# Weight sums of a seven-product matmul moved to the stages before it, and its first row tiles prepared inside the last block of the product before

## The chip, the cores and the metric

The kernel runs on one core of a Trainium2 chip. The metric is the device time of one execution in microseconds (us); three timed executions of the kernel before stand below, and beside them one execution with a profile. The engines are TensorE (PE, with its weight loads PEld), VectorE (DVE), ScalarE (ACT), GpSimd (POOL) and the queue of SyncE (SP). DMAs are issued by SP, POOL and ACT.

## The reference

One layer of a hybrid decoder, for 1024 prompt positions and 8 samples of one position (1032 tokens), all in fp32:

```python
    z = x @ w_in + b_in                      # 1024 -> 3584
    y_a = s5_mixer(u_a, ...)                 # scan, GELU, GLU
    y_b = u_b * spatial_mix(layer_norm(v_b), sgu_w, sgu_b)
    merged = (jax.nn.sigmoid(gate_a) * (y_a @ w_branch_a)
              + jax.nn.sigmoid(gate_b) * (y_b @ w_branch_b))
    mix = merged @ w_out + b_out
    x1 = layer_norm(DN_ALPHA * x + mix, ln1_g, ln1_b)
    ff = jnp.square(jax.nn.relu(x1 @ w_up + b_up)) @ w_down + b_down
    ple = jax.nn.sigmoid(x1 @ w_ple_gate + b_ple_gate) * (p @ w_ple)
    x2 = layer_norm(DN_ALPHA * x1 + ff + ple, ln2_g, ln2_b)
```

`w_up` is 1024 x 4096 and `w_down` 4096 x 1024; the change lies around these two products.

## The kernel before

**Layout and precision.** Features lie on the 128 partitions, tokens along the free axis: a tile is 128 x 1032, a half of it 516, a quarter 258. Every fp32 operand is split into a high part (a copy that rounds, mostly on ACT) and a low part (a subtraction on DVE), and a product is three matmuls: high by high, high by low, low by high. Weights come through the pool `raw` (loaded by SP), are split into the pool `hl` of four buffers, and the splits run three weight tiles ahead of PE.

**Stages.** In order: `w_in` (to about 380 us, with the scan beside it), `glu` (four tiles, to 410.6), `pab` (the two branch products, eight times a product `psB` and a product `psA` of 36 matmuls each, to about 505), `out` (twice eight), `pg` and `ple`, then from 715.1 the first feed-forward product ("up"), from 1069.6 the second ("down"), and a normalisation that ends at 1422. In `pab` the sum of a tile m is `sb = psB * sb; sa = psA * sa; sa = sa + sb` on DVE, then a split; the two PSUM buffers alternate, so the `psA` of the next tile needs this tile's `sa = psA * sa` done.

**The two feed-forward products** use a scheme of seven products in the place of eight block products (P1 to P7). Up runs 16 blocks `up_pair(p)`. A block is seven products of 24 matmuls (168 in all) into three PSUM regions; its four weight tiles (t = 0 to 3) are `w_up` pieces and sums of pieces, made on DVE by `up_prep`. Some products add into a region that holds an earlier one: P6, P7 and P4 go onto P1, so P4 may start only when DVE has read the result of P7 (`hB[:, 1]`, line 1314). Each block's result h goes, as seven operands, into DRAM tiles `hd` through POOL's queue.

**Down** runs seven products of four units `dn_unit(pi, mp)` of 96 matmuls. Its row operands (`hop`, 23 buffers) are loaded from `hd` into `hraw` (four buffers) by SP, and split. Its weights are pieces of `w_down` and the sums S1 to S4 of such pieces, which `dn_sums` forms: eight steps of four loads of 512 KB (SP), four DVE operations of 128x1024 and four stores of 512 KB to DRAM (POOL). One step of the generator is taken at each product of up (`next(dsums, None)`). The residual `acc`, parked in DRAM (`accd`), is loaded again by SP before down starts, and the result of P1 is added to it in P1.

**What sets the order.** Each engine and each DMA queue does its instructions in the order of the program that the tile framework's scheduler wrote; a tile whose buffer is taken again waits for the last reader, a DMA included.

Of the kernel before, what the change touches and what calls it, by code (L numbers as in the profile page):

```python
# [10 lines left out]
F32 = mybir.dt.float32  # L11
# [46 lines left out]
def hybrid_step_kernel(ctx: ExitStack, tc: tile.TileContext, i, o):  # L58
# [7 lines left out]
    rawp = ctx.enter_context(tc.tile_pool(name="raw", bufs=4))  # L66
# [843 lines left out]

    yhl += [(unit(f"A{8 + 2 * m}", F32R, name=f"yh{m + 2}"), unit(f"A{9 + 2 * m}", F32R, name=f"yl{m + 2}"))
# [5 lines left out]
    for m in range(4):  # L917
# [9 lines left out]
        split(yb[m][0], yb[m][1], ubt[m])  # L927

# [15 lines left out]
    for m in range(8):  # L944
# [11 lines left out]
        mg.append((a, b))  # L956

# [125 lines left out]
    lnx = bpool.tile([128, 1024], F32, tag="dsz", name="lnx")  # L1083
# [30 lines left out]
    for j, (p_, m) in enumerate(passes):  # L1114
# [83 lines left out]
    UPO = [("P1", 0, C5), ("P5", 0, D5), ("P6", 1, C5), ("P3", 1, D5), ("P7", 2, C5), ("P2", 2, D5),  # L1198
# [13 lines left out]
    def up_prep(n):  # L1212

        p, t = n // 4, n % 4
        if t == 0:
            ra, rb, rc, rd = (raw_() for _ in range(4))
            upr[p] = (ra, rb, rc, rd)
            nc.sync.dma_start(out=ra[:, C5], in_=i["w_up"][p][:, C5])
            nc.sync.dma_start(out=rd, in_=i["w_up"][p + NP])
            nc.sync.dma_start(out=rc[:, D5], in_=i["w_up"][p][:, D5])  # L1220
        ra, rb, rc, rd = upr[p]
        if t == 0:
            tt(V, ra[:, D5], rd[:, C5], rd[:, D5], ALU.add)
# [18 lines left out]

    sd = {n: [dram.tile([128, 1024], F32, tag=f"{n}d{k}", name=f"{n}d{k}") for k in range(8)]
          for n in ("S1", "S2", "S3", "S4")}

    def dn_load(r_, m, j, kh):
        n = 2 * j + kh
        if n == 3:
            nc.sync.dma_start(out=r_, in_=i["w_dl"][m])
        else:  # L1250
            for g in range(2):
                nc.sync.dma_start(out=r_[:, 512 * g:512 * g + 512],
                                  in_=i["w_down"][(2 * n + g) * 4 + m // 2][
                                      :, (m % 2) * 512:(m % 2) * 512 + 512])

    def dn_sums():
        for k in range(8):
            mp, kh = k // 2, k % 2
            x, y = (unit(free[8 + t], F32, [128, 1024], name="dsum") for t in range(2))
            z = bpool.tile([128, 1024], F32, tag="dsz", name="dsz")  # L1260
            dn_load(x, mp + 4, 0, kh)
            dn_load(y, mp + 4, 1, kh)
            dn_load(z, mp, 0, kh)
            for _ in range(5):
                yield
            tt(V, y, x, y, ALU.add)
            nc.gpsimd.dma_start(out=sd["S1"][k], in_=y)  # L1267
            yield
            tt(V, x, z, x, ALU.subtract)
            nc.gpsimd.dma_start(out=sd["S3"][k], in_=x)  # L1270
            yield
            tt(V, z, y, z, ALU.subtract)
            nc.gpsimd.dma_start(out=sd["S2"][k], in_=z)
            y = unit(free[9], F32, [128, 1024], name="dsum")
            dn_load(y, mp, 1, kh)
            for _ in range(3):
                yield
            tt(V, y, y, z, ALU.subtract)
            nc.gpsimd.dma_start(out=sd["S4"][k], in_=y)
            for _ in range(3):  # L1280
                yield

    dsums = dn_sums()

    def up_pair(p):
# [53 lines left out]
    for _ in dsums:  # L1339
        pass  # L1340
    pools_free = [f"A{k}" for k in range(16)] + ["T0", "T1"] + [f"B{k}" for k in range(20)]
    acc2tags = ["A3", "A7"] + [b1tags[1, k] for k in range(4)] + ["B12", "B17"]
    rest = [t_ for t_ in pools_free if t_ not in acc2tags]
    utags, rtags, ntags = rest[0:2], rest[2:6], rest[7:]
    otag = rest[6]
    NH = len(ntags)
    acc = []
    for m in range(8):
        u = unit(acc2tags[m], name=f"acb{m}")
        nc.sync.dma_start(out=u, in_=accd[m])  # L1350
        acc.append(u)
    us = [unit(utags[k], F32, [128, 2, HF], name=f"us{k}") for k in range(2)]
    usl = [us[m // 2][:, m % 2] for m in range(4)]
# [34 lines left out]
    def h_prep(n):  # L1388
# [3 lines left out]
        u = unit(ntags[n % NH], F32R, [128, 2, HF], name="hop")  # L1392
        src = hraw[n // 2][:, n % 2]
# [6 lines left out]
        if n % 2:  # L1400
            hraw.pop(n // 2)
            h_load(n // 2 + 1)
            h_load(n // 2 + 2)
            h_load(n // 2 + 3)

    def h_ahead(n):
        while hn[0] <= min(n, 111):
            h_prep(hn[0])
# [14 lines left out]
    def dn_unit(pi, mp):  # L1423
        pr = DNO[pi]
        ps = region2()
        for k in range(16):
# [41 lines left out]
    h_ahead(NH - 1)  # L1468
# [9 lines left out]
    accp = [acc[m] for m in perm]  # L1478

    def ln_last(t0, n, step_):  # L1480
# [4 lines left out]
        xs_ = [s_[:, sl] for s_ in accp]  # L1485
# [217 lines left out]
```

## Time and profile before

| what | value |
|---|---|
| three timed runs | 1424.95, 1428.08 (median), 1428.72 us |
| the profiled execution | 1424.12 us, its span 1422.2 us |
| PE busy | 1366.1 us (96%) |
| DVE busy | 928.8 us (65%) |
| ACT busy | 457.1 us (32%) |
| HBM read and written | 160.72 MB and 68.16 MB |
| mean granted clock of PE | 0.986 of full speed |

PE is the engine that is nearly always busy, so the places where it is not, and the places where its clock is granted lower, are where time can be had or lost. A busy share says nothing of an engine that is waited for at one place only; the waits of PE and the counts of matmuls in equal stretches do.

### The profile page before, as it was taken

The numbers are of one execution on the slowest core, as the hardware profiler recorded it, in microseconds if no ns is written. First come the engines' busy times: TensorE is split into PE (matmuls) and PEld (weight loads), VectorE is DVE, ScalarE is ACT, GpSimd is POOL, SyncE is SP. The second block draws the span as 40 slices with busy tenths as digits, with TensorE's granted clock in tenths as the row PEclk, the third lists the DMA queues.
The fourth block names the chain that finished last, engine by engine and source line by source line (L and its number), as shares of the span: only waits on it lengthen the run. The fifth ranks groups of instructions, "written<-read, shape, count | busy, mean of one in ns | idle before, by whom it ended". The sixth has DMA issues, their size and how long they took to land.

```text
span 1422.2 us, 24852 instructions
## 1 busy us (share of the span) xinstructions
PE 1366.1 (96%) x10302; PEld 1354.6 (95%) x10302; DVE 928.8 (65%) x1488; ACT 457.1 (32%) x616; POOL 143.3 (10%) x214
## 2 busy tenths in 40 slices
PE   8999999999999999999998989999988999999995
PEld 8999899999999999999998979999988999999995
DVE  7929349215765546996887877767756654666857
ACT  3231231133241134562232222223333432344423
POOL 0320310103500000000011212111100000000000
PEclk9999999999999999999999999999998999999998
DMA  7572673531214444423278888644379754665421
GB/s 267 141 187 84 160 151 96 144 136 46 83 57 151 138 123 134 123 88 135 86 249 305 307 277 303 222 158 149 120 262 341 253 159 143 214 214 178 144 81 60
DMA packets 105026, 237.20 MB, mean 167 GB/s; under 512 B 11064, under 2 KB 35528, under 8 KB 104912
## 3 DMA queue, kind: packets, MB, share of 16 engines
q1 hardware_dynamic: 84480, 181.11, 40.2%
q0 software_dynamic: 15344, 51.08, 10.2%
q10 hardware_dynamic: 5088, 3.42, 1.1%
q8 instruction: 81, 1.33, 0.4%
q14 instruction: 33, 0.27, 0.1%
HBM read 160.72 MB, written 68.16 MB: 161 GB/s over the span
## 4 chain that ended last, share of the span: by engine, by line
PE 64%; issue 13%; DVE 12%; DMA 7%; POOL 2%; ACT 1%; SPq 0%; ACTq 0%; POOLq 0%; DVEq 0%
PE q L1077 19%; PE q L1437 18%; PE big L143 11%; DVE tb L83 3%; PE big L120 2%; PE big L122 2%; PE big L121 2%; DMA dsum<-w_down 2%; DVE hl L83 1%; POOL hd L1323 1%; DMA L<-Sst 1%; DMA raw<-w_up 1%; DVE H L83 1%; PE q L1421 1%; PE q L1420 1%
## 5 line engine op out<-in xcount | busy, mean ns | idle before, releaser
L83 DVE TENSOR_TENSOR hl<-raw,hl 128x1024 fp32r<-128x1024 f32 (+1 forms) x189 | 221.5, 1175 | 134.5 <-ACT hl L106 133.6
L106 ACT ACTIVATE hl<-raw 128x1024 fp32r<-128x1024 f32 (+1 forms) x187 | 190.5, 1020 | 324.2 <-PE q L1437 112.5
L1437 PE MATMUL q<-hop,hl 128*128 128x258 f32 x2304 | 280.9, 284 | 4.5 <-DVE hop L1395 3.8
L1437 PEld LDWEIGHTS q<-hop,hl 128*128 128x128 f32 x2304 | 279.8, 191 | 5.3 <-DVE hop L1395 4.0
L1077 PE MATMUL q<-xb,hl 128*128 128x258 f32 x1920 | 241.5, 283 | 0.2 <-ACT p L1307 0.2
L1077 PEld LDWEIGHTS q<-xb,hl 128*128 128x128 f32 x1920 | 235.9, 190 | 0.6 <-ACT p L1307 0.4
L1077 PE MATMUL q<-xT,hl 128*128 128x258 f32 x1536 | 199.2, 289 | 22.0 <-DVE hB L80 21.3
L1077 PEld LDWEIGHTS q<-xT,hl 128*128 128x128 f32 x1536 | 193.3, 195 | 24.2 <-DVE hB L80 22.9
L120 PE MATMUL big<-xh,hl 128*128 128x344 f32 x512 | 165.9, 324 | 1.0 <-ACT uab L293 1.0
L122 PE MATMUL big<-xh,hl 128*128 128x344 f32 x512 | 163.7, 320 | 0.0
L121 PE MATMUL big<-xl,hl 128*128 128x344 f32 x512 | 163.4, 319 | 0.0
L120 PEld LDWEIGHTS big<-xh,hl 128*128 128x128 f32 x512 | 96.2, 188 | 1.8 <-ACT uab L293 1.3
L122 PEld LDWEIGHTS big<-xh,hl 128*128 128x128 f32 x512 | 96.2, 188 | 0.0
L121 PEld LDWEIGHTS big<-xl,hl 128*128 128x128 f32 x512 | 96.2, 188 | 0.0
L1077 PE MATMUL q<-mgh,hl 128*128 128x258 f32 x512 | 83.6, 285 | 1.4 <-DVE sa L83 1.4
L83 DVE TENSOR_TENSOR hop<-hraw,hop 128x516 fp32r<-128x516 f32 x112 | 72.0, 689 | 12.7 <-ACT hop L1397 12.5
L1077 PEld LDWEIGHTS q<-mgh,hl 128*128 128x128 f32 x512 | 71.0, 190 | 1.8 <-ACT hl L106 1.7
L1397 ACT ACTIVATE hop<-hraw 128x516 fp32r<-128x516 f32 x90 | 54.0, 629 | 41.9 <-DMA hraw<-hd 36.4
L83 DVE TENSOR_TENSOR raw<-raw 128x512 f32<-128x512 f32 x64 | 43.3, 688 | 28.4 <-DMA raw<-w_up 28.1
L1077 PE MATMUL q<-mgl,hl 128*128 128x258 f32 x256 | 51.4, 282 | 0.0
L716 ACT ACTIVATE sg<-big,vec 128x1032 f32<-128x1032 f32 x16 | 18.0, 1125 | 96.3 <-issue 55.7
L1267 POOL DMA_DIRECT2D S1d<-dsum x8 | 4.4, 554 | 376.8 <-DVE dsum L83 376.8
(327 smaller groups left out, 1905.7 us busy)
## 6 DMA issues: line engine op xcount, KB each, us to landing
hraw<-hd SPq DMA_DIRECT2D x56, 516.0 KB, 5.1
gd<-sg SPq DMA_DIRECT2D x16, 516.0 KB, 4.0
hd<-hB POOLq DMA_DIRECT2D x16, 516.0 KB, 4.9
hd<-tA POOLq DMA_DIRECT2D x16, 516.0 KB, 5.4
hd<-tB POOLq DMA_DIRECT2D x16, 516.0 KB, 6.0
raw<-w_gate SPq DMA_DIRECT2D x16, 512.0 KB, 4.8
raw<-w_out SPq DMA_DIRECT2D x16, 512.0 KB, 3.6
raw<-w_pg SPq DMA_DIRECT2D x16, 512.0 KB, 3.6
```

The costliest lines, as they stand in the source:

```text
L83: eng.tensor_tensor(out=out, in0=a, in1=b, op=op)
L106: S.activation(out=hi, in_=src, func=AF.Copy)
L120: T.matmul(out, wh, xh[:, sl], start=(start and k == 0), stop=False)
L121: T.matmul(out, wh, xl[:, sl], start=False, stop=False)
L122: T.matmul(out, wl, xh[:, sl], start=False, stop=(stop and k == last))
L143: T.matmul(ps[:, t, 0:TT], w_, x_[:, t * TT:(t + 1) * TT], start=st_, stop=sp_)
L716: S.activation(out=f3(sg), in_=fv(ps), func=AF.Sigmoid, bias=col("b_ga" if m < 8 else "b_gb", m % 8))
L1077: T.matmul(ps[:, j, 0:QT], w_, x_[:, j * QT:(j + 1) * QT], start=st_, stop=sp_, skip_group_check=True)
L1323: put = lambda q, n, src: nc.gpsimd.dma_start(out=d_[q:q + n, p % 2].rearrange("q p n -> p q n"), in_=src)
L1397: S.activation(out=u[:, 0, :], in_=src, func=AF.Copy)
L1420: T.matmul(r_, wh, xl_, start=False, stop=False, skip_group_check=True)
L1437: T.matmul(ps[:, j, 0:QT], w_, x_[:, quarter(j)], start=st_, stop=sp_, skip_group_check=True)
```

## The change

The sums S1 to S4 are formed in 16 smaller steps of 128x512 (`sums_in` loads four pieces through POOL's queue, `sums_out` does four DVE operations and four stores through POOL). They stand in `glu` (before tile 0 and after tiles 1 and 3), after each tile of `pab`, at two tiles of `out`, and in the first five blocks of up. A step's loads are held back by a copy of one column from a tile of the current block into the load's target, and its sums by a copy of one column into a gate tile. In up the pool `raw` has three buffers in the place of four, the fourth piece (`rd`) goes into tiles of another pool, the order of the seven products is another, and part of the relu and square goes from DVE to ACT. In the last block the first 16 row tiles of down are loaded and split, each held back by a column of that block. The residual is loaded by POOL during P1 and P2 of down, and P1's result is added to it in P2.

```diff
-    rawp = ctx.enter_context(tc.tile_pool(name="raw", bufs=4))
+    rawp = ctx.enter_context(tc.tile_pool(name="raw", bufs=3))
...
+    def sums_in(after):
+        if nq[0] == 16:
+            return
+        n = nq[0]
+        mp, kh, g = n // 4, n // 2 % 2, n % 2
+        nq[0] += 1
+        ts_ = [bpool.tile([128, HF], F32, tag=f"ds{t}", name="dsum")[:, 0:512] for t in range(4)]
+        for t, m, j in ((0, mp + 4, 0), (1, mp + 4, 1), (2, mp, 0), (3, mp, 1)):
+            V.tensor_copy(out=ts_[t][:, 0:1], in_=after)
+            dn_load(ts_[t], m, j, kh, (g,), nc.gpsimd)
+        quad.append((n, ts_))
+    def sums_out(after):
...
+        n, (x, y, z, w) = quad.pop()
+        V.tensor_copy(out=gate_, in_=after)
+        V.memset(gate_, 1.0)
+        stt(V, y, x, gate_, y, ALU.mult, ALU.add)
+        tt(V, x, z, x, ALU.subtract)
+        tt(V, z, y, z, ALU.subtract)
+        tt(V, w, w, z, ALU.subtract)
+        for nm, t in (("S1", y), ("S3", x), ("S2", z), ("S4", w)):
+            nc.gpsimd.dma_start(out=sd[nm][n // 2][:, 512 * (n % 2):512 * (n % 2) + 512], in_=t)
+    sums_in(ubt[3][:, 0:1])
...
+        if m % 2:
+            sums_out(sg[:, 0:1])
+            sums_in(sg[:, 0:1])
...
+        sums_out(sa[:, 0:1])
+        sums_in(sa[:, 0:1])
...
-    UPO = [("P1", 0, C5), ("P5", 0, D5), ("P6", 1, C5), ("P3", 1, D5), ("P7", 2, C5), ("P2", 2, D5),
+    UPO = [("P1", 0, C5), ("P2", 0, D5), ("P6", 1, C5), ("P5", 1, D5), ("P7", 2, C5), ("P3", 2, D5),
            ("P4", 3, D5)]
...
-            ra, rb, rc, rd = (raw_() for _ in range(4))
+            ra, rb, rc = (raw_() for _ in range(3))
+            rd = unit(free[8 + p % 2], F32, [128, 1024], name="rawu")
...
-            nc.sync.dma_start(out=ra[:, C5], in_=i["w_up"][p][:, C5])
+            nc.sync.dma_start(out=ra, in_=i["w_up"][p])
             nc.sync.dma_start(out=rd, in_=i["w_up"][p + NP])
-            nc.sync.dma_start(out=rc[:, D5], in_=i["w_up"][p][:, D5])
...
+        if last:
+            for n in range(4):
+                h_load(n)
...
-            next(dsums, None)
...
+                if last:
+                    h_ahead(7, u2s[:, 0:1])
...
             elif nm == "P3":
                 stt(V, h2(hA[:, 1]), r_, b1, h2(u2s), ALU.add, ALU.add)
+                S.activation(out=hA[:, 1], in_=hA[:, 1], func=AF.Relu)
+                S.activation(out=hA[:, 1], in_=hA[:, 1], func=AF.Square)
             else:
-                S.activation(out=h2(hB[:, 0]), in_=r_, func=AF.Identity, bias=b2)
-                stt(V, hB, hB, 0.0, hB, ALU.max, ALU.mult)
+                S.activation(out=h2(hB[:, 0]), in_=r_, func=AF.Relu, bias=b2)
+                S.activation(out=hB[:, 0], in_=hB[:, 0], func=AF.Square)
...
+    def acc_in(m, after):
+        u = unit(acc2tags[m], name=f"acb{m}")
+        V.tensor_copy(out=u[:, 0:1], in_=after[:, 0:1])
+        nc.gpsimd.dma_start(out=u, in_=accd[m])
+        acc[m] = u
...
-    def h_prep(n):
+    def h_prep(n, after=None):
...
+        if after is not None:
+            V.tensor_copy(out=u[:, 0, 0:1], in_=after)
...
         if pr == "P1":
             S.activation(out=h2(u), in_=r_, func=AF.Copy)
-            stt(V, h2(A1[:, q1]), r_, b1, h2(A1[:, q1]), ALU.add, ALU.add)
-        elif pr == "P2":
-            add(A1[:, q1])
...
+        elif pr == "P2":
+            stt(V, h2(A1[:, q1]), r_, b1, h2(A1[:, q1]), ALU.add, ALU.add)
+            tt(V, A1[:, q1], A1[:, q1], u, ALU.add)
+            acc_in(mp + 4, A1)
...
+    for p in range(NP):
+        up_pair(p)
+        u = last_of[ptags[0]][:, 0, 0:1]
+        sums_out(u)
+        sums_in(u)
```

In `pab`, on DVE, one tile of the loop of before reads as follows (`sb` and `sa` are the gates that are multiplied by the two products in `big`, `hl` a weight split, `mgl` the low part of the merged tile):

```order
L83 TENSOR_TENSOR sb_3945<-big_4038,sb_3945 128x1032
L83 TENSOR_TENSOR sa_3944<-big_4076,sa_3944 128x1032
L83 TENSOR_TENSOR hl_4119<-raw_3852,hl_4119 128x1024
L83 TENSOR_TENSOR sa_3944<-sa_3944,sb_3945 128x1032
L83 TENSOR_TENSOR mgl2_4116<-sa_3944,mgh2_4115 128x1032
```

The same stretch of DVE with the change (`dsum` are the four pieces, a `COPY` of 128x1 into one is the hold on its next load, `tie` the gate tile):

```order
L86 TENSOR_TENSOR sb_3944<-big_4059,sb_3944 128x1032
L86 TENSOR_TENSOR dsum_3924<-dsum_3923,dsum_3924 128x512
L86 TENSOR_TENSOR dsum_3925<-dsum_3925,dsum_3924 128x512
L942 COPY dsum_4039<-sa_3934 128x1
L942 COPY dsum_4038<-sa_3934 128x1
L942 COPY dsum_4040<-sa_3934 128x1
L86 TENSOR_TENSOR sa_3943<-big_4097,sa_3943 128x1032
L942 COPY dsum_4041<-sa_3934 128x1
L86 TENSOR_TENSOR hl_4162<-raw_3818,hl_4162 128x1024
L86 TENSOR_TENSOR sa_3943<-sa_3943,sb_3944 128x1032
L951 COPY tie_3667<-sa_3943 128x1
L952 MEMSET tie_3667 128x1
```

Three of the four copies into the pieces (`dsum_4039`, `4038`, `4040`), whose buffers the stores of the step before still read, stand in front of `sa = psA * sa`.

At the start of up, DVE in the kernel before has these rows after the last residual sum but two (`hl_6953` is the split of the weights for t = 1, the third and fourth product of block 0):

```order
L83 TENSOR_TENSOR acc3_5621<-acc3_5621,q_6765 128x516
L83 TENSOR_TENSOR hl_6948<-raw_6940,hl_6948 128x1024
L83 TENSOR_TENSOR acc3_5621<-acc3_5621,q_6779 128x516
L83 TENSOR_TENSOR hl_6953<-raw_6941,hl_6953 128x1024
L80 SCALAR_TENSOR_TENSOR acc3_5621<-pre3_4572,acc3_5621 128x1032
```

With the change the split of the weights for t = 1 (`hl_7216`) stands behind the residual's last tile (`acc7`, `pre7`), the operands `xT` of the last group and three sums of `w_up` pieces (`raw_7206`, `raw_7207`, from `rawu_7208`):

```order
L86 TENSOR_TENSOR acc7_5922<-acc7_5922,q_7156 128x516
L83 SCALAR_TENSOR_TENSOR acc7_5922<-pre7_4841,acc7_5922 128x1032
...
L942 COPY dsum_7438<-pu_7200 128x1
L86 TENSOR_TENSOR raw_7206<-rawu_7208 128x512
L86 TENSOR_TENSOR raw_7207<-raw_7205,rawu_7208 128x512
L86 TENSOR_TENSOR raw_7206<-raw_7206,raw_7205 128x512
L111 CAST xT4_3_7185<-pre7_4841 128x516
L86 TENSOR_TENSOR raw_7207<-raw_7205,raw_7206 128x512
L86 TENSOR_TENSOR xT4_3_7185<-pre7_4841,xT4_3_7185 128x516
L86 TENSOR_TENSOR hl_7216<-raw_7206,hl_7216 128x1024
```

The split moved from in front of `acc3`'s last step to behind `acc7`'s, and behind the cast of `xT4`.

## Rows read from the trace of the kernel before

**Rows 1.** part 1 of the page: busy time, share of the span, instructions

```profile
PE 1366.1 (96%) x10302; PEld 1354.6 (95%) x10302; DVE 928.8 (65%) x1488; ACT 457.1 (32%) x616; POOL 143.3 (10%) x214
```

**Rows 2.** waits of PE over the span: us in total, times, longest

```profile
PE q L1077 <- DVE hB L80: 21.3, 8, 5.2
...
PE q L1437 <- DVE hop L1395: 3.8, 1, 3.8
PE big L303 <- DVE hl L83: 2.4, 2, 1.9
```

**Rows 3.** windows by engine: up, one full block of it, 50 us of down

```profile
core 0: us, PE busy (x) PEld busy (x) DVE busy (x) ACT busy (x) POOL busy (x), PEclk, DMA share, GB/s
715.10:1069.60 354.50, 332.27 (x2690) 329.80 (x2689) 256.04 (x312) 101.39 (x135) 57.83 (x92) 0.98 0.69 236
948.00:968.00 20.00, 20.00 (x169) 20.00 (x168) 13.21 (x17) 6.09 (x8) 2.50 (x4) 1.00 0.39 138
1100.00:1150.00 50.00, 50.00 (x417) 50.00 (x417) 28.27 (x37) 20.51 (x27) 0.00 (x0) 1.00 0.64 217
```

**Rows 4.** windows, same columns, 1080 to 1090 in the start of down

```profile
1080.00:1085.00 5.00, 1.05 (x4) 0.72 (x3) 1.64 (x3) 0.64 (x1) 0.00 (x0) 0.77 1.02 401
1085.00:1090.00 5.00, 4.42 (x22) 4.42 (x23) 4.63 (x6) 1.72 (x4) 0.00 (x0) 0.54 1.04 398
```

**Rows 5.** waits of DVE in up, and the DMAs of 740 to 900

```profile
DVE raw L83 <- DMA raw<-w_up: 28.1, 15, 3.7
...
DVE dsum L83 <- DMA dsum<-w_down: 14.8, 5, 4.7
...
DMA packets 16821, 48.06 MB, mean 300 GB/s; under 512 B 1906, under 2 KB 1906, under 8 KB 16807
```

**Rows 6.** a tile of pab: its window, then DVE's timeline (start, us)

```profile
427.70:439.00 11.30, 11.30 (x73) 11.30 (x73) 5.86 (x6) 2.13 (x2) 0.00 (x0) 1.00 0.45 141
...
478.87 1.23 DVE L83 TENSOR_TENSOR sa<-big,sa 128x1032 f32<-128x1032 f32 x1 [4.30 <-PE big L143]
480.02 1.22 DVE L83 TENSOR_TENSOR hl<-raw,hl 128x1024 fp32r<-128x1024 f32 x1
483.52 1.23 DVE L83 TENSOR_TENSOR mgl<-sa,mgh 128x1032 fp32r<-128x1032 f32 x1 [1.14 <-ACT mgh L106]
...
490.19 1.23 DVE L83 TENSOR_TENSOR sa<-big,sa 128x1032 f32<-128x1032 f32 x1 [4.30 <-PE big L143]
```

**Rows 7.** page part 5, one group: busy, mean ns, idle before it

```profile
L83 DVE TENSOR_TENSOR raw<-raw 128x512 f32<-128x512 f32 x64 | 43.3, 688 | 28.4 <-DMA raw<-w_up 28.1
```

**Rows 8.** DMA issues (KB each, median us to landing) of 740 to 900; landings of tile hA

```profile
S2d<-dsz POOLq DMA_DIRECT2D x7, 512.0 KB, 5.6
...
hd<-hA POOLq DMA_DIRECT2D x6, 258.0 KB, 3.1
...
DMA to landing us min/median/max: 2.6/3.0/6.3
```

**Rows 9.** POOL and DVE in up, timelines (start, us, instruction)

```profile
726.65 1.23 DVE L83 TENSOR_TENSOR dsum<-dsz,dsum 128x1024 f32<-128x1024 f32 x1
...
728.18 0.54 POOL L1270 DMA_DIRECT2D S3d<-dsum  x1 [0.70 <-DVE dsum L83]
```

**Rows 10.** the start of up: timelines of PE, DVE and SP

```profile
715.10 3.05 PE L1077 MATMUL q<-xb,hl 128*128 128x258 f32 x24
...
718.06 0.33 SPq L1186 DMA_DIRECT2D accd<-acc  x1
...
722.71 0.43 DVE L108 CAST xT<-pre 128x516 fp32r<-128x516 f32 x1 [0.71 <-DMA accd<-acc]
723.05 1.22 DVE L83 TENSOR_TENSOR hl<-raw,hl 128x1024 fp32r<-128x1024 f32 x1
```

**Rows 11.** page part 6: KB each, median us to landing

```profile
hraw<-hd SPq DMA_DIRECT2D x56, 516.0 KB, 5.1
...
hd<-hB POOLq DMA_DIRECT2D x16, 516.0 KB, 4.9
```

More of the change, by code (lines that the diff above doesn't have):

```diff
@@ L908, in hybrid_step_kernel, with dn_load @@
         tt(V, ubt[h], sgt[h], ubt[h], ALU.mult)
+    sd = {n: [dram.tile([128, 1024], F32, tag=f"{n}d{k}", name=f"{n}d{k}") for k in range(8)]
+          for n in ("S1", "S2", "S3", "S4")}
+    def dn_load(r_, m, j, kh, gs=(0, 1), eng=nc.sync):
+        n = 2 * j + kh
+        if n == 3:
+            c = slice(512 * gs[0], 512 * gs[-1] + 512)
+            eng.dma_start(out=r_, in_=i["w_dl"][m][:, c])
+        else:
+            for k, g in enumerate(gs):
+                eng.dma_start(out=r_[:, 512 * k:512 * k + 512],
+                              in_=i["w_down"][(2 * n + g) * 4 + m // 2][
+                                  :, (m % 2) * 512:(m % 2) * 512 + 512])
+    gate_ = bpool.tile([128, 1], F32, tag="tie", name="tie")
+    quad = []
+    nq = [0]
+    def sums_in(after):
[10 more added lines that the diff above has]
+    def sums_out(after):
+        if not quad:
+            return
+        n, (x, y, z, w) = quad.pop()
[8 more added lines that the diff above has]
+    sums_in(ubt[3][:, 0:1])
     yhl += [(unit(f"A{8 + 2 * m}", F32R, name=f"yh{m + 2}"), unit(f"A{9 + 2 * m}", F32R, name=f"yl{m + 2}"))
@@ L1127, in hybrid_step_kernel @@
         if p_ == 0 and m == 7:
+            lnx = bpool.tile([128, HF], F32, tag="ds0", name="lnx")
             lnq.add(ln_half(pre, 0, ssum, tmpu, lnx, "ln1_g", "ln1_b", x1_split))
@@ L1240, in hybrid_step_kernel @@
     ptags, htags = free[0:2], (free[2:4] + free[6:8], free[4:6] + free[6:8])
[L1243 to L1283, printed above, removed]
     def up_pair(p):
@@ L1293, in up_pair @@
         a, c, b = region2(), region2(), region2()
+        d_ = hd[p // 2]
+        put = lambda q, n, src: nc.gpsimd.dma_start(
+            out=d_[q:q + n, p % 2].rearrange("q p n -> p q n"), in_=src)
         ps = {"P1": a, "P6": a, "P7": a, "P4": a, "P5": c, "P3": c, "P2": b}
+        last = p == NP - 1
+        if last:
+            for n in range(4):
+                h_load(n)
         for nm, t, cs_ in UPO:
             up_ahead(4 * p + t + 3)
-            next(dsums, None)
             w = wq[4 * p + t]
@@ L1332, in up_pair @@
         put(5, 2, tB)
-    for p in range(NP):
-        up_pair(p)
+        if last:
+            h_ahead(15, tB[:, 1, 0:1])
     DNO = ["P1", "P2", "P6", "P7", "P4", "P5", "P3"]
[L1339 to L1348, printed above, removed]
+    rtags = [free[8], free[2], free[3], free[9]]
+    tagof = {id(u): t_ for t_, u in last_of.items()}
+    lasts = [tagof[id(u)] for n in ("11", "21", "T2", "T1", "T3", "22", "T4") for u in xq[n]]
+    NH = 23
+    ntags = lasts[0:NH]
+    rest = lasts[NH:]
+    acc2tags = [free[0], free[1], free[4], free[5], free[6], free[7]] + rest[0:2]
+    utags, otag = rest[2:4], rest[4]
+    acc = [None] * 8
+    def acc_in(m, after):
         u = unit(acc2tags[m], name=f"acb{m}")
[L1350 to L1353, printed above, removed]
+        V.tensor_copy(out=u[:, 0:1], in_=after[:, 0:1])
+        nc.gpsimd.dma_start(out=u, in_=accd[m])
+        acc[m] = u
+    us, usl = [], []
     wn = [0]
@@ L1401, in h_prep, with h_ahead @@
             hraw.pop(n // 2)
[L1402 to L1406, printed above, removed]
+            for j in range(1, 4):
+                if n > 15 or n // 2 + j < 8:
+                    h_load(n // 2 + j)
+    def h_ahead(n, after=None):
         while hn[0] <= min(n, 111):
-            h_prep(hn[0])
+            h_prep(hn[0], after)
             hn[0] += 1
@@ L1425, in dn_unit @@
         ps = region2()
+        if pi == 0 and mp == 0:
+            us.extend(unit(utags[k], F32, [128, 2, HF], name=f"us{k}") for k in range(2))
+            usl.extend(us[k // 2][:, k % 2] for k in range(4))
         for k in range(16):
```

60 lines of the change are left out of this document (39 added, 21 removed).

## The prediction

> **What bounds the kernel now.** The page's busy shares come first: PE is busy for 96% of a span of 1422.2 us, DVE for 65% [rows 1]. So time is to be had only where PE stands still or runs at a lower granted clock. The list of PE's waits says where that is: 21.3 us of PE's idle time lie in up, in eight waits for `hB`, and 3.8 us lie at one `hop` in the start of down [rows 2].
>
> The size comes from counting matmuls in windows, since this catches the lower clock too. In 50 undisturbed microseconds of down PE did 417 matmuls at full clock, which is 0.1199 us each; the block of up at 948 did 169 in 20.0 us, the same rate [rows 3]. A block has 168, so it should last 20.1 us, and 16 blocks 2688 x 0.1199 = 322.3 us. Up lasts 354.5 us [rows 3]. It loses 32.2 us.
>
> Why: in up DVE waits 28.1 us for `w_up` pieces and 14.8 us for `dsum` pieces, while the DMAs move 300 GB/s [rows 5]. DVE works in order, so an evacuation (`hB`) that stands behind such a wait is late, and P4 cannot start. The block at 948, which is one without losses, had 138 GB/s [rows 3]: where there is little traffic, nothing is lost.
>
> In the start of down, 1080 to 1090 held 4 + 22 matmuls at granted clocks of 0.77 and 0.54 [rows 4], where 10 / 0.1199 = 83.4 would fit: 57.4 x 0.1199 = 6.9 us lost, because the row operands are loaded only when up has ended. Together 39.1 us can come back.
>
> **The change part by part.**
>
> *What it removes.* Of the 16 new steps of the sums, each with eight DMAs of 256 KB (2.1 MB), four remain in up (steps formed in blocks 0 to 4). In those blocks the traffic is that of the block at 948 plus about 2.1 MB per 20.1 us (104 GB/s): 138 + 104 = 242 GB/s. Later blocks fall back to 138. The former waits came at 300, so I take all 32.2 us as gone, and the 6.9 us too, as the first 16 row tiles are then split before down. DVE has room: 13.2 us busy per 20 us [rows 3], to which a step adds 4 x 0.69 = 2.8 us [rows 7], and part of the relus leaves for ACT, which has 6.1 us of 20 in use [rows 3]. What is late next in a block is again DVE's evacuation, if its loads still come late (a rival below). Bounds of the gain: 39.1 above, and 17 if up stays starved.
>
> *What it adds in pab*, the term I am least sure of. A step moves 2.1 MB per tile; a tile of `pab` moved 141 GB/s with DVE busy 5.9 of 11.3 us [rows 6], so the traffic rises to about 330 GB/s. Three hold copies stand on DVE in front of `sa = psA * sa`, which frees the PSUM buffer. Each waits until a store of the step before has left its tile, so a tile's loop now runs through DVE, POOL and a DMA. From `sa`'s start to `mgl`'s start DVE needs 483.52 - 478.87 = 4.65 us [rows 6]; the fourth copy is an estimated 0.1; `mgl` and `sb` go at 480.02 - 478.87 = 1.15 each [rows 6]; between and behind them two sums, one at an estimated pitch of 0.61 and the last at 0.69 [rows 7]. That is 4.65 + 0.1 + 1.15 + 0.61 + 1.15 + 0.69 = 8.35 us to the end of S2. From a sum's end to POOL's issue it is 728.18 - (726.65 + 1.23) = 0.30 us [rows 9]; I add 0.2 for the copies themselves. So a loop lasts 8.9 us + L, where L is the time of a 256 KB store from issue to landing. PE's tile lasts 490.19 - 478.87 = 11.32 us [rows 6]; if the loop is longer, the difference is paid in each of seven tiles, and once more in what the first tile's wait exceeds its slack, about L - 2.6. The two PSUM buffers delay this loss inside `pab`, but `out` begins in the same banks, so it comes due there.
>
> For L the nearest row is the store of `hA`: 258 KB on the same queue, at the same traffic, 3.1 us; its least and greatest are 2.6 and 6.3, and the `S2d` store of 512 KB took 5.6 [rows 8]. At 3.1 the loop is 12.0, 0.68 x 7 + 0.5 = 5.3 us. At 2.6 it is 0.18 x 7 = 1.3 us; at 4.0, 1.58 x 7 + 1.4 = 12.5; at 5.6, 3.18 x 7 + 3.0 = 25. I take 5.3, and keep 1.3 and 25 for the range. A waiting copy also holds back the weight split `hl` and the sum of `sa` behind it; their users have their own slack of several microseconds (DVE's 4.3 us wait for PE before `sa` [rows 6]).
>
> The row for L stands on its own; beside it, the Trainium skill, "DMA: Bandwidth & Descriptors", section "Anatomy of one DMA — SWDGE (gpsimd) path", gives a transfer of POOL's queue as about 2.0 us + bytes / 436 GB/s. For 256 KB that makes 2.6 us as an estimate, and the term would be 1.3 us. The trace agrees for its least store only; its median is 0.4 to 0.5 us longer.
>
> *What it adds at the start of up.* The weights of t = 1 (`hl_7216`) need the piece in `rawu`, whose tile is free only after the last `ple` matmul, where up begins (715.1), and they stand on DVE behind the residual and the cast of `xT4`. In before that cast waited for the store of `accd` and ran at 722.71, 7.6 us into up [rows 10]; the store is still there. Behind the cast come a sum, the low part of `xT4`, and `hl_7216` (pitches of 0.35, 0.61, 0.61, then 1.15 to its end): 715.1 + 7.6 + 2.7, ready 10.3 us into up. The third product asks for it after 48 x 0.1199 = 5.8 us, and its matmuls with the high part give about 1 us of cover. 10.3 - 5.8 - 1.0 = 3.5 us. Bounds: nothing, if the cast comes sooner, and 5.2, the longest wait that up has shown [rows 2].
>
> *What it adds in the last block.* The first row tiles of down are loaded and split inside block 15, in front of evacuations on DVE and ACT. Their data of block 14 need its `hB` store (issued 2.3 us after that block's last sum begins: four pitches of 0.61), 4.9 us to land, and a load of 5.1 us [rows 11]: 12.3 us into block 15. The splits of up to six such rows at an estimated 0.69 each (the sum of about this size [rows 7]) stand in front of `hB`'s evacuation of some 0.75: 17.2 us into the block. P4 starts at 144 x 0.1199 = 17.3. That is a tie: I put 1.0 us, with bounds 0 and 5.2 [rows 2].
>
> *The rest.* In `glu` the step of the sums and the eight issues fit beside PE, as DVE there has the same kind of slack. `raw` with three buffers lets a load start one tile later; the only weight wait of the early stages is 2.4 us in two pieces [rows 2]. I put 0.5 us, with bounds 0 and 2.4. The residual's loads in P1 and P2 lie beside a PE-bound stage (50.00 of 50 us busy [rows 3]) and cost nothing; if that cover were gone, it is one wait at P2's end, some 3 us.
>
> *Sum*, against the profiled execution of 1424.1 us: - 39.1 + 5.3 + 3.5 + 1.0 + 0.5 = - 28.8, so 1395.3. That execution lies 4.0 us below the median of the timed runs (1428.08), their fastest at 1424.95; I add half of this difference: 1397.
>
> **The rivals.**
>
> *A: the stores of pab land late, L about 5 to 5.6.* For it: four stores, four loads and a weight load share the DMAs in one tile, and the row for 512 KB has 5.6 [rows 8]. Against it: 258 KB stores at 300 GB/s took 3.1. Time: 5.3 becomes 25, or 20.5 at L = 5: 1397 + 15 to 20, about 1414.
>
> A rule of the Trainium skill speaks for A: "SBUF — State Buffer", section "Who interferes with whom", says that a DVE copy in a two-port mode locks GpSimd out of the port through which it writes descriptors. The rows here have a POOL issue of 0.54 us beside running DVE sums [rows 9], so it does not show for sums; whether it does for the copies no row shows.
>
> *B: up stays starved.* In blocks 0 to 4 loads are late as before, or a block's own order (the seven products are reordered) has its evacuations late; about 1.4 us per block, as before on average half of (354.5 - 322.3) / 16 = 2.0. For it: DVE's order still puts sums that wait for DMA before evacuations. Against it: the block at 948. Time: 1397 + 16 x 1.3, about 1418.
>
> *C: nothing new is waited for.* The stores land at 2.6 us and the starts of up and of down are covered: 1424.1 - 39.1 + 2 = 1387.
>
> *D: slower.* One mechanism: L in `pab` beyond 7.2 us. Each tile then pays over 4.8 us and the term is 33.5 + 4.6 = 38 us, which with 5.0 for the other costs outweighs the gain of 39.1 by over 0.3%. At L = 7.7 the term is 5.28 x 7 + 5.1 = 42 us: 1424 - 39 + 42 + 5 + 2 = 1434. For it: the greatest landing of `hA` was 6.3 [rows 8], and a wait for three stores takes the slowest. Against it: it would need such a landing in every tile.
>
> *E: the change does nothing*, as the losses in up turn up again in `pab` to the same sum (L near 6.7): 1428.
>
> **How the numbers follow.** Forecast 60%, A 14%, B 9%, C 8%, E 4%, D 5%. A difference below about 0.3% (4.3 us) can't be told from none here. Faster by more: 60 + 14 + 9 + 8 = 91%; within: 4%; slower: 5%. The forecast's own range is 1390 to 1404 (L of 2.6 to 4.0). The range that is to hold the time 8 times in 10 takes in C's end and A's and B's: 1386 to 1417.
>
> **What would show it.** Right: blocks of up every 20.1 us, no gap at the start of down, a gap of some 3 us of PE for `hl` about 6 us into up, and in `pab` DVE's hold copies ending a wait for the S2 store just before `sa`, with a loss of some microseconds at the first matmuls of `out`. Wrong: waits for `hB` in up, or a pitch of `pab` tiles of 13 us and more. The forecast fails most easily at L.

## The result, and the profile after

The changed kernel took 1408.95 us in the median of four runs (1405.81 to 1411.36), the kernel before 1428.4; the ratio is 0.9864, with a 95% interval of 0.9835 to 0.9893. It is faster by 1.4%, where 1397 (2.2%) was forecast. The profiled execution is the slowest of the four (1411.36 us, span 1409.4), that of before (1424.12 us) is faster than each of its timed runs; between the two spans lie 12.8 us, between the medians 19.4. The accounts below are made between the profiles.

The first look is at where the stages begin. These rows tell the first and last start of the matmuls of a tile; first before, then after (`ybh` opens `pab`, `mgh` opens `out`, `ph` ends ahead of up, `hop` opens down):

```profile
L143 PE MATMUL big<-ybh,hl x192: 315/319/325, 410.6 to 495.5; 128*128 128x344 f32 x192
L1077 PE MATMUL q<-mgh,hl x512: 278/283/472, 502.9 to 597.2; 128*128 128x258 f32 x171
L1077 PE MATMUL q<-ph,hl x128: 279/283/290, 651.3 to 715.0; 128*128 128x258 f32 x128
L1437 PE MATMUL q<-hop,hl x2304: 276/283/583, 1069.6 to 1356.2; 128*128 128x258 f32 x192
```

```profile
L146 PE MATMUL big<-ybh,hl x192: 314/319/492, 410.1 to 503.2; 128*128 128x344 f32 x192
L1134 PE MATMUL q<-mgh,hl x512: 277/283/552, 514.1 to 610.1; 128*128 128x258 f32 x171
L1134 PE MATMUL q<-ph,hl x128: 279/283/290, 664.3 to 727.9; 128*128 128x258 f32 x128
L1476 PE MATMUL q<-hop,hl x2304: 276/283/473, 1065.4 to 1344.2; 128*128 128x258 f32 x192
```

| stretch | before | after | difference | forecast |
|---|---|---|---|---|
| to `pab` | 410.6 | 410.1 | -0.5 | +0.5 |
| `pab` | 92.3 | 104.0 | +11.7 | +5.3 |
| `out` to up | 212.1 | 213.8 | +1.7 | 0 |
| up | 354.6 | 337.5 | -17.1 | -32.2 + 3.5 + 1.0 = -27.7 |
| down and the end | 352.6 | 344.0 | -8.6 | -6.9 |
| sum | 1422.2 | 1409.4 | -12.8 | -28.8 |

So the gain is where it was looked for, and two stages give back more than was priced. The waits of PE after (us in total, times, longest) name the places; they answer to [rows 2]:

```profile
PE q L1134 <- DVE dsum L942: 4.9, 1, 4.9
PE q L1134 <- DVE hB L83: 4.5, 2, 2.4
PE q L1134 <- ACT hl L109: 3.5, 1, 3.5
PE big L146 <- DVE sb L86: 3.4, 3, 1.9
```

The eight waits for `hB` (21.3 us) have become two (4.5), and the wait for `hop` in down is gone. New are the waits for a `dsum` copy of line 942, the hold on a step's loads (the 4.9 us stand at the first matmuls of `out`), those for `sb` in `pab`, and one for `hl` at the start of up. The windows of up after, with the columns of [rows 3], show what such a wait costs with the clock behind it:

```profile
728.00:748.00 20.00, 16.50 (x116) 16.29 (x115) 15.97 (x27) 6.33 (x8) 2.69 (x5) 0.83 0.64 212
788.00:808.00 20.00, 17.91 (x137) 17.70 (x136) 14.98 (x24) 7.18 (x12) 6.93 (x12) 0.91 0.62 221
848.00:868.00 20.00, 20.00 (x168) 20.00 (x168) 12.01 (x16) 9.04 (x13) 2.73 (x4) 1.00 0.42 140
1048.00:1065.40 17.40, 15.01 (x113) 14.80 (x112) 13.28 (x33) 10.88 (x19) 0.57 (x1) 0.90 0.91 311
```

At 0.1199 us a matmul, 20 us hold 166.8 and 17.4 us hold 145.1. The first window lost 50.8 matmuls (6.1 us) for a wait of 3.5, the one at 788 29.8 (3.6 us) for a wait of 2.1, the last 32.1 (3.8 us) for a wait of 2.4: 13.5 us for 8.0 us of waits. The other blocks run at their full 168 in some 20 us, as the window at 848 does.

In `pab`, DVE's timeline of one tile (start, us, instruction, in brackets the idle time before it and what ended it) shows the predicted order:

```profile
447.45 1.23 DVE L86 TENSOR_TENSOR sa<-big,sa 128x1032 f32<-128x1032 f32 x1
...
458.97 0.15 DVE L942 COPY dsum<-sa 128x1 f32<-128x1 f32 x1 [1.90 <-DMA S1d<-dsum]
460.10 0.15 DVE L942 COPY dsum<-sa 128x1 f32<-128x1 f32 x1 [0.98 <-DMA S3d<-dsum]
460.78 0.15 DVE L942 COPY dsum<-sa 128x1 f32<-128x1 f32 x1 [0.53 <-DMA S2d<-dsum]
460.88 1.23 DVE L86 TENSOR_TENSOR sa<-big,sa 128x1032 f32<-128x1032 f32 x1
...
512.75 1.23 DVE L86 TENSOR_TENSOR sa<-big,sa 128x1032 f32<-128x1032 f32 x1
```

Three copies wait for three stores, and `sa` comes right behind them, 13.43 us after the last `sa`. From 447.45 to 512.75 there are five tiles: 13.06 us each, where PE needs 11.32 [rows 6]. The loss goes on into `out`, where the clock stood lower behind the wait of 4.9 us:

```profile
514.00:530.00 16.00, 15.87 (x117) 15.90 (x118) 10.92 (x19) 5.26 (x6) 4.97 (x10) 0.87 0.82 277
```

16 us hold 133.4 matmuls, so 16.4 are missing there, 2.0 us; `out` to up is 1.7 us longer than before.

### The profile page after: what moved, and what is told of

It reads as the page before. It is cut to its first block, busy times and chain, and to the rows that moved or that the text cites. A ratio compares the mean times of both kernels' runs of the same rounds, so it can differ in the third digit from the quotient of the medians.

```text
span 1409.4 us, 25105 instructions
## 1 busy us (share of the span) xinstructions
PE 1365.3 (97%) x10302; PEld 1355.4 (96%) x10302; DVE 923.2 (65%) x1631; ACT 503.2 (36%) x696; POOL 200.2 (14%) x318
## 4 chain that ended last, share of the span: by engine, by line
PE 74%; DVE 12%; DMA 8%; issue 3%; POOL 2%; ACT 1%; SPq 0%; ACTq 0%; DVEq 0%; POOLq 0%
PE q L1134 34%; PE q L1476 19%; PE big L146 5%; DVE tb L86 3%; PE big L123 2%; PE big L125 2%; PE big L124 2%; DMA dsum<-w_down 2%; DVE hl L86 1%; DMA S4d<-dsum 1%; DVE H L86 1%; DMA L<-Sst 1%; PE q L1455 1%; PE q L1456 1%; PE q L1457 1%
## 5 line engine op out<-in xcount | busy, mean ns | idle before, releaser
L86 DVE TENSOR_TENSOR hl<-raw,hl 128x1024 fp32r<-128x1024 f32 (+1 forms) x173 | 210.8, 1221 | 193.0 <-ACT hl L109 192.7
L1476 PE MATMUL q<-hop,hl 128*128 128x258 f32 x2304 | 277.6, 283 | 0.0
L109 ACT ACTIVATE hl<-raw 128x1024 fp32r<-128x1024 f32 x171 | 180.4, 1056 | 232.2 <-PE q L1476 114.7
L1134 PE MATMUL q<-xb,hl 128*128 128x258 f32 x1920 | 238.0, 283 | 0.0
L1134 PE MATMUL q<-xT,hl 128*128 128x258 f32 x1536 | 195.8, 288 | 8.0 <-DVE hB L83 4.5
L925 POOL DMA_DIRECT2D dsum<-w_down x48 | 25.8, 540 | 217.0 <-DVE dsum L942 216.5
L83 DVE SCALAR_TENSOR_TENSOR hA<-q,vec,pu 128x516 f32<-128x516 f32 x32 | 24.1, 754 | 38.5 <-issue 22.3
```

The lines of the kernel that those rows point to most:

```text
L83: eng.scalar_tensor_tensor(out=out, in0=in0, scalar=sc, in1=in1, op0=op0, op1=op1)
L86: eng.tensor_tensor(out=out, in0=a, in1=b, op=op)
L109: S.activation(out=hi, in_=src, func=AF.Copy)
L925: eng.dma_start(out=r_[:, 512 * k:512 * k + 512], in_=i["w_down"][(2 * n + g) * 4 + m // 2][:, (m % 2) * 512:(m % 2) * 512 + 512])
L1134: T.matmul(ps[:, j, 0:QT], w_, x_[:, j * QT:(j + 1) * QT], start=st_, stop=sp_, skip_group_check=True)
L1476: T.matmul(ps[:, j, 0:QT], w_, x_[:, quarter(j)], start=st_, stop=sp_, skip_group_check=True)
```

## The experiments

Each kernel ran beside the kernel before on the same chip; ratios are to it, with 95% intervals.

**The holds on GpSimd.**

```diff
-            V.tensor_copy(out=ts_[t][:, 0:1], in_=after)
+            nc.gpsimd.tensor_copy(out=ts_[t][:, 0:1], in_=after)
```

> The column copies that hold back a step's loads are done by GpSimd in the place of VectorE; all else is as in the changed kernel. Theory (the copies stand on VectorE in front of the evacuation of psA and of hB): the pitch of a pab tile goes from 13.1 us back to about 11.4, pab from 104.0 to 92-95 us, the wait of 4.9 us at the start of out goes, and the hB wait of 2.1 us in block 3 of up goes with it; the whole falls by 10 to 17 us, to 1392-1399 us. Rival (traffic: the pieces and weights come late whoever waits for the stores, or the 2.8 us of sums per tile are the cost): pab stays above 100 us and the whole at 1404 or more.

Measured: 1412.38 us, ratio 0.9911 (0.9884 to 0.9937); `pab` from 410.7 to 520.2, 109.5 us. The theory fell and the rival's numbers came (`pab` above 100 us, the whole above 1404): the copies are gone from DVE, and `pab` is longer. DVE now waits for the pieces themselves, once a tile, 13.7 us apart:

```profile
455.54 0.75 DVE L83 SCALAR_TENSOR_TENSOR dsum<-dsum,tie 128x512 f32<-128x512 f32 x1 [3.65 <-DMA dsum<-w_down]
...
469.25 0.75 DVE L83 SCALAR_TENSOR_TENSOR dsum<-dsum,tie 128x512 f32<-128x512 f32 x1 [3.52 <-DMA dsum<-w_down]
```

That suggested another theory: with one set of four buffers, loads, sums, stores and the next loads form a ring, and it is longer than a tile wherever its wait stands.

**Half the steps in `pab`.**

```diff
-        sums_out(sa[:, 0:1])
-        sums_in(sa[:, 0:1])
+        if m % 2:
+            sums_out(sa[:, 0:1])
+            sums_in(sa[:, 0:1])
```

> In pab a step of the sums is taken after every second tile (four steps in the place of eight); the four others follow in up, in eight or nine blocks in the place of four. Loop theory: with one set of four buffers a step's loads, sums and stores and the next step's loads are a ring of 13 to 15 us, whoever does the holding, and a tile lasts 11.3; given two tiles (22.6 us), the ring costs nothing: pab falls from 104.0 to 92-95 us, the wait at the start of out goes, up grows by 0 to 4 us, the whole is 1396-1401. Rival (each step costs about 1.7 us wherever it stands in pab, by its traffic and its 2.8 us of VectorE): pab is 97-99 and the whole about 1403-1407.

Measured: 1390.5 us, ratio 0.9761 (0.9723 to 0.98). `pab` is 92.2 us (410.8 to 503.0), up 330.6. The ring theory's number for `pab` came in; up, which was to grow by 0 to 4 us, fell by 6.9, and with it the whole came out below the 1396 to 1401. But half the steps are also half the traffic, so one more run was needed.

**Two sets of buffers.**

```diff
+        if n in (3, 5, 7, 9):
+            us_ = [unit(f"T{t}", name="dsum") for t in range(2)]
+            ts_ = [us_[t // 2][:, 512 * (t % 2):512 * (t % 2) + 512] for t in range(4)]
...
```

> As the changed kernel, a step of the sums after every tile of pab, but every second step takes its four pieces in two tiles that are idle there, so that two sets of buffers alternate: traffic and work per tile are those of the changed kernel (279 GB/s), and a ring of loads, sums and stores has two tiles' time. Loop theory: pab falls from 104.0 to 92-95 us as with half the steps, the wait at the start of out goes, the whole is 1391-1398. Rival (the traffic of a step per tile makes pieces, gates and weights late): pab is 99 or more and the whole 1403 or more.

Measured: 1397.2 us, ratio 0.9791 (0.9766 to 0.9815); `pab` 92.2 us again (409.8 to 502.0). Here every tile has its step, as in the changed kernel. Its window in `pab`, then its stores there (KB each, median us to landing), and those of the changed kernel:

```profile
433.00:500.00 67.00, 67.00 (x428) 67.00 (x428) 53.16 (x90) 13.21 (x13) 24.92 (x47) 1.00 0.93 324
```

```profile
S1d<-dsum POOLq DMA_DIRECT2D x7, 256.0 KB, 5.3
S3d<-dsum POOLq DMA_DIRECT2D x7, 256.0 KB, 6.5
S2d<-dsum POOLq DMA_DIRECT2D x7, 256.0 KB, 6.0
```

```profile
S1d<-dsum POOLq DMA_DIRECT2D x7, 256.0 KB, 6.0
S3d<-dsum POOLq DMA_DIRECT2D x7, 256.0 KB, 4.0
S2d<-dsum POOLq DMA_DIRECT2D x7, 256.0 KB, 3.0
```

PE does 428 matmuls in 67 us without a gap, at 324 GB/s and with stores that mostly land later than in the changed kernel. The traffic was not the cost; the ring without slack was. (In this kernel the holds also stand behind `sa`; the run with the holds on GpSimd shows that this alone does not help.)

**All sums in up.** The calls in `glu`, `pab` and `out` are taken out; the 16 steps stand in the 16 blocks.

> All 16 steps of the sums are taken in up, one per block, none in glu, pab and out; the order of the products, the smaller steps and all else are as in the changed kernel. It asks what took up's losses away: fewer sums in up, or the new form of its blocks. Theory 1 (fewer sums; each block with a step loses like before, about 2 us): pab returns to 92.4 us and the start of out to no wait (-13 us), up grows by about 24 us to 361: 1418-1422. Theory 2 (a step of the new form costs a block only its hold copies, as in one of the four blocks with steps, 1 us per block): up 349, whole 1406-1410. Theory 3 (the new block does not mind the sums): up 338-341, whole 1395-1400.

Measured: 1404.78 us, ratio 0.9864 (0.9832 to 0.9895), the same ratio as the changed kernel's; `pab` 92.2 us (409.5 to 501.7), up 338.8. That is theory 3 for up; the whole missed its 1395 to 1400, as down and the end took 348.5 us in the place of 344.0. So a block of the new form can carry a step and keep its pace. This does not say that moving the sums was idle: in the kernel before, blocks without a step run at full rate with all relus on VectorE, as the one at 948 does [rows 3]. Three runs ask what in the new form lets a block with a step keep its pace.

**Relus back on VectorE, all sums in up.**

```diff
-                S.activation(out=hB[:, 1], in_=hB[:, 1], func=AF.Relu)
-                S.activation(out=hB[:, 1], in_=hB[:, 1], func=AF.Square)
...
-                S.activation(out=hA[:, 1], in_=hA[:, 1], func=AF.Relu)
-                S.activation(out=hA[:, 1], in_=hA[:, 1], func=AF.Square)
+                stt(V, hA[:, 1], hA[:, 1], 0.0, hA[:, 1], ALU.max, ALU.mult)
...
-                S.activation(out=h2(hB[:, 0]), in_=r_, func=AF.Relu, bias=b2)
-                S.activation(out=hB[:, 0], in_=hB[:, 0], func=AF.Square)
+                S.activation(out=h2(hB[:, 0]), in_=r_, func=AF.Identity, bias=b2)
+                stt(V, hB, hB, 0.0, hB, ALU.max, ALU.mult)
```

> The kernel with all 16 small steps in up, and the relu and square of h back on VectorE as in the kernel before (about 3 us per block). If VectorE's room is what the new block lives on, hB's evacuations are late again: up grows from 338.8 to 348-356, the whole to 1411-1419. If the order of the products or the size of the steps does it, up stays at 337-342 and the whole at 1401-1407.

**Loads of the pieces by SyncE, all sums in up** (`nc.gpsimd` becomes `nc.sync` in `sums_in`).

> The kernel with all 16 small steps in up, and the loads of their pieces issued by SyncE in the place of GpSimd. Queue theory: the waits for stores hold up the loads of w_up again, and up grows from 338.8 to 348-358 us, the whole to 1411-1420. Rival (form of the blocks): up stays at 337-342, the whole at 1401-1407.

**The kernel before, loads of the pieces by GpSimd** (`nc.sync` becomes `nc.gpsimd` in `dn_sums`).

> The kernel before with one edit: the 32 loads of pieces for its sums are issued by GpSimd in the place of SyncE. All sums stay in up, in their eight large steps. Queue theory: on SyncE's queue these loads wait some 78 us in all for the stores of the step before, and the loads of w_up stand behind them; freed of that, up falls from 354.5 to 335-342 us and the whole by 12 to 18. Rival (it was the form of the blocks: the order of the products, the relus on VectorE, steps of 512 KB): up stays above 350 us and the whole within 4 us of before.

Measured: relus on VectorE 1430.11 us, 1.0027 (1.001 to 1.0045); loads by SyncE 1409.66, 0.9909 (0.9879 to 0.9939); before with loads by GpSimd 1422.88, 0.9993 (0.9976 to 1.001). The first went past the 1411 to 1419 of its theory, the second lies between its two theories, and the third did what its rival said. The same 296 us of up in the four kernels, in the order in which they stand here from "all sums in up", and in before:

```profile
734.00:1030.00 296.00, 292.24 (x2429) 291.82 (x2428) 220.91 (x381) 130.81 (x190) 104.30 (x178) 1.00 0.72 249
```

```profile
734.00:1030.00 296.00, 272.79 (x2184) 270.30 (x2183) 219.34 (x368) 78.80 (x105) 94.45 (x160) 0.97 0.66 222
```

```profile
734.00:1030.00 296.00, 286.68 (x2342) 285.01 (x2341) 213.29 (x368) 123.36 (x181) 71.01 (x116) 0.98 0.70 238
```

```profile
734.00:1030.00 296.00, 282.37 (x2296) 280.93 (x2295) 219.91 (x265) 83.61 (x110) 79.43 (x134) 0.98 0.70 240
```

```profile
734.00:1030.00 296.00, 278.11 (x2258) 276.24 (x2258) 216.69 (x262) 82.19 (x110) 52.22 (x84) 0.98 0.67 233
```

296 us hold 2469 matmuls. With all sums in up 40 are missing (4.8 us), at the highest traffic of the five (249 GB/s); with the relus back on VectorE 285 (34 us); with the loads by SyncE 127 (15 us); in before 211 (25 us), and with its loads by GpSimd 173 (21 us). So with a step in every block it is the relus on ACT that keep the pace. The new order of the products and the smaller steps alone do not: the version with its relus back has both, and loses more than the kernel before. What they add beside the relus no run separates. The queue of the loads is a smaller cause, if it is one: the profile with the loads by SyncE is the slowest of its five runs and that of "all sums in up" the fastest of its four, the intervals of the two ratios overlap, and in the kernel before the same exchange shows nothing in the time. What VectorE waits for from 715 to 1040 in the version with its relus back (us in total, times, longest), then with all sums in up:

```profile
DVE dsum L942 <- DMA S1d<-dsum: 30.5, 12, 3.0
DVE dsum L942 <- DMA S2d<-dsum: 28.4, 12, 4.4
DVE dsum L942 <- DMA S3d<-dsum: 7.1, 11, 1.3
```

```profile
DVE dsum L942 <- DMA S3d<-dsum: 28.6, 13, 4.4
DVE dsum L942 <- DMA S2d<-dsum: 12.0, 12, 2.1
...
DVE dsum L942 <- DMA S4d<-dsum: 8.5, 12, 1.4
```

With the relus back, VectorE's work is 219.34 us for 2184 matmuls, 16.9 per block of 168. Such a block lasted 296 / 13 = 22.8 us, so 325 us are 14.3 blocks, and the 66.0 us of waits are 4.6 in each: 21.5 us, where PE needs 20.1. With the relus on ACT the work is 220.91 / 2429 x 168 = 15.3, and the 49.1 us of waits over 15.9 blocks are 3.1: 18.4 us. In this pair the block keeps its pace where VectorE's work and its waits together fit into it.

**A filled gap.** 30 matmuls of ready operands stand in front of the third product of block 0.

```diff
+            if p == 0 and nm == "P6":
+                w0 = wq[0]
+                for k in range(30):
+                    T.matmul(c[:, k % 2, 0:QT], w0[:, 0, 0:128], xq["11"][0][:, 0, 0:QT], start=True, stop=True,
+                             skip_group_check=True)
```

> 30 matmuls of ready operands into a PSUM region that the fourth product overwrites are put in front of the third product of up's first block, where PE stood still for 3.5 us. They change no result. Theory (a standstill is paid twice, once itself and once in a lower granted clock behind it): in the first 20 us of up the clock stays at 1.00, where it was 0.83, the 24 matmuls of the third product take 2.9 us, and up falls by about 2.5 us although PE does 3.6 us of needless work. Rival (the clock fell for another reason, the work or traffic of that stretch): the clock stays near 0.83, and up is as long as before or up to 1 us longer.

Measured: 1406.51 us, ratio 0.9864 (0.9841 to 0.9886), which the time alone can't tell from the changed kernel. The first 20 us of up:

```profile
727.00:747.00 20.00, 19.19 (x159) 18.98 (x158) 17.53 (x29) 6.23 (x8) 2.69 (x5) 1.00 0.68 218
```

The clock stays at 1.00; 159 - 30 = 129 useful matmuls stand against 116, 1.6 us more, although 3.6 us of needless work are in it. The theory holds in its direction; in these 20 us the size is 1.6 us, not 2.5 (a wait of 0.8 was left).

**No rows at P5 in the last block** (`h_ahead(11, ...)` is taken out there).

> In the last block of up the four row tiles that were prepared at P5 are prepared after P7's evacuation. Theory (hB's evacuation stands on VectorE behind a row cast that waits for its load, 3.35 us): PE's wait of 2.4 us before P4 in the last block goes, and with it the low clock behind it; up falls from 337.4 by 2.5 to 4 us, the whole by about 3. Rival (the rows are then late for down): a wait for a row of the same size appears at the start of down, up falls but the whole stays within 1 us.

Measured: 1408.09 us, ratio 0.9876 (0.9848 to 0.9904). PE's wait for `hB` in the last block fell from 2.39 to 1.20 us, without a low clock, and down shows a wait of 0.18; but in this profile the wait in block 3 was 3.40 us. The edit does half of what was expected, and its time alone shows nothing.

**Versions made from this.** The first takes 15 steps in up and none in `pab`, loads block 0's fourth piece early into two idle buffers, and prepares rows 4 to 13 of down behind P7's evacuation. The others take a step after every second tile of `pab` with the same early load, one with rows 8 to 11 behind P7's evacuation and one with rows 4 to 11.

```diff
+                rd = tuple(bpool.tile([128, HF], F32, tag=f"ds{1 + k}", name="rawu")[:, 0:512] for k in range(2))
...
-                if last:
-                    h_ahead(11, p5[:, 0:1])
```

> A version meant to be faster than both: one step of the sums before glu, none in pab and out, 15 in up; the first block's fourth piece is loaded into two idle buffers of the sums, ahead of up; in the last block only rows 0 to 3 are prepared before P7's evacuation, the others behind it. If the gaps at up's start (3.7 us and the low clock behind it, 6.3 in all) and in the last block (about 9 us) are what these two edits remove, up is 324-330 us after 338.8, the start of down loses no more than 2 us, and the whole is 1386-1392. Rival: a gap moves to the next late thing (an operand of the residual at up's start, rows 8 to 13 at down's start), up 332-336, the whole 1396-1402.

> A step after every second tile of pab, the first block's fourth piece loaded early into idle buffers, and rows 8 to 11 prepared behind P7's evacuation in the last block. If the gains add: up 324-326 us (330.6 less the 4 us lost at its start and 1 to 2 at its end), down 344-345, the whole 1382-1386. Rival: the last block still waits some 1.2 us for hB, and the start of up for another operand: 1387-1391.

> As b3a, and rows 4 to 7 are also prepared behind P7's evacuation. If the evacuation is then free of every row: up 323-325; the price is a wait of some 1.9 us at the start of down, as in the version with all steps in up: the whole 1382-1387, within 2 us of b3a.

Measured: 1388.38 us, 0.9753 (0.972 to 0.9787); 1387.72, 0.9728 (0.9707 to 0.9748); 1386.25, 0.9718 (0.9695 to 0.974). The first and the last lie in what was expected; the second came out at its rival's, with a wait of 1.6 us for `hB` left in the last block. The last two can't be told apart by time. The waits of PE from up on in the last one:

```profile
PE q L1481 <- DVE hop L1436: 1.6, 1, 1.6
```

Up takes 323.5 us there (715.0 to 1038.5), against 322.3 without any loss. These versions beat both kernels.

## Why the prediction was right, and where its terms were not

The direction, the stages and the range held; the gain was 19.4 us of the 31 forecast. The range that held, 1386 to 1417, was to take in rivals A and B too. The forecast's own range, 1390 to 1404, did not hold, and the time is nearer to A's 1414 than to 1397. Of the prediction's own signs of being wrong, one came in full, a pitch of `pab` tiles of 13 us, and one in part, two waits for `hB` in up.

*What can come back.* The 39.1 us were all there: the best version's up (323.5), and down's 344.0 after the change, show it. The mechanism, an evacuation late behind VectorE's waits, held, and taking the sums out of a block is one way to end it, as the block at 948 shows [rows 3]. Traffic as the condition did not hold: all sums in up, at 249 GB/s, lost 4.8 us of 296, and the relus back on VectorE lost 34 at 222. What the prediction counted as a side effect, the relus on ACT, is a second way, by which a block keeps its pace with its step. In the changed kernel it can matter in the four blocks that form a step; at 34 / 13 = 2.6 us a block that is some 10 us, an estimate. The other twelve blocks have no step.

*`pab`*, the term named as the least sure: forecast 5.3, measured 11.7, and 1.7 more in `out`, where the lower clock of 514 to 530 alone is 2.0 us, which the term did not have. The loop through the hold copies is in the trace, 13.06 us a tile where 12.0 was taken. Its S2 store, from issue to hold copy, took 4.75, 4.05, 4.29, 3.11 and 2.41 us in the five tiles, 3.7 in the mean and not 3.1; the first of the five is this issue, with the copy at 460.78 above:

```profile
456.03 0.54 POOL L958 DMA_DIRECT2D S2d<-dsum  x1 [1.20 <-DVE dsum L86]
```

The rest is a wait that the loop of the prediction did not have, for the loads of the pieces in front of a sum. It made three of the five tiles 0.34, 1.30 and 1.62 us longer, 0.65 in the mean; the last of them:

```profile
507.51 0.69 DVE L86 TENSOR_TENSOR dsum<-dsum 128x512 f32<-128x512 f32 x1 [1.53 <-DMA dsum<-w_down]
```

With 8.7 us for the fixed part, where 8.9 was taken, this is 8.7 + 3.7 + 0.65 = 13.05. So a median of 3.1 us was not wrong for a store (the seven S2 stores have 3.0), but the loop adds up the late ones and the late loads. The hold's place was not the point either, as the first experiment shows.

The estimate of 2.6 us a store from the Trainium skill ("DMA: Bandwidth & Descriptors", "Anatomy of one DMA — SWDGE (gpsimd) path") was further off: here the medians are 3.0 to 6.0 us, and the measurement decides. The lock on GpSimd's port, which rival A borrowed from the Trainium skill ("SBUF — State Buffer", "Who interferes with whom"), is not shown by any run; GpSimd's store above took 0.54 us to issue, as the one of [rows 9] did.

*The three gaps in up.* The start: 3.5 forecast, 3.5 us of wait measured, but 6.1 lost. That the waits agree is partly luck, for the cause was partly another: the piece itself came 6.4 us after its issue, and the cast of `xT4`, which the forecast had late, ran behind it without a wait, as SyncE's and DVE's timelines show. With the piece loaded early, in the best version, the gap is gone.

```profile
727.99 1.30 SPq L1281 DMA_DIRECT2D rawu<-w_up  x2
```

```profile
734.42 0.69 DVE L86 TENSOR_TENSOR raw<-rawu 128x512 f32<-128x512 f32 x1 [1.50 <-DMA rawu<-w_up]
...
736.24 0.42 DVE L111 CAST xT<-pre 128x516 fp32r<-128x516 f32 x1
...
1056.65 0.43 DVE L1431 CAST hop<-hraw 128x516 fp32r<-128x516 f32 x1 [3.35 <-DMA hraw<-hd]
...
1060.29 0.75 DVE L83 SCALAR_TENSOR_TENSOR hB<-q,vec,p 128x516 f32<-128x516 f32 x1
```

The last block: 1.0 forecast, 2.4 of wait, 3.8 lost, by a row cast in front of `hB`'s evacuation as predicted, one that itself waited 3.35 us for its load (the last two lines). Block 3, where a hold waited in front of `hB`: nothing forecast, 3.6 lost. Each was priced by its wait alone, and the lower clock behind it added 13.5 - 8.0 = 5.5 us.

*Down* with the end gained 8.6 against 6.9 (no run separates the other 1.7), and the residual added a product later shows no wait of PE, as forecast.

## What to carry to other kernels

Where a step loads, computes and stores through one set of buffers, compare its whole ring with the period of the loop that it stands in; if it is longer, moving the wait to another engine doesn't help, a second set or half the rate does. An engine that works in order can be full through its work and its waits together, even at 74% busy (219.34 of 296 us); less work on it or fewer waits then help alike. Price a gap of a few microseconds of TensorE with the clock that follows it.

## What the runs showed of the hardware

After a wait the granted clock did not fall every time. The timelines of PE in the version with the relus on VectorE (a product of 24 matmuls lasts 3.15 us at full clock):

```profile
761.35 3.16 PE L1128 MATMUL q<-xT,hl 128*128 128x258 f32 x24 [2.79 <-DVE dsum L942]
...
854.62 4.52 PE L1128 MATMUL q<-xT,hl 128*128 128x258 f32 x24 [1.85 <-DVE hB L83]
```

A product behind a wait of 1.85 us took 1.4 us longer, one behind 2.79 us did not. The time of one kernel varies with it: the changed kernel's four runs had mean clocks of 0.985 to 0.990 and lay 5.6 us apart, while the best version, with hardly a wait left, lay within 0.6 us.
